# Smaller first loads over three queues, and another order of rounding and transposing in the first stretch of a two-layer decoder kernel

## The chip, the core and the metric

The kernel runs on one NeuronCore of one Trainium2 chip. Its engines work from queues of their own, each strictly in order: TensorE (PE: matmuls and transposes, with PEld its weight loads), VectorE (DVE), ScalarE (ACT), GpSimd (POOL) and SyncE (SP, which here only issues DMAs). ScalarE and GpSimd can issue DMAs too. The metric is device time in microseconds.

## The reference

Two layers of a decoder trunk over 512 tokens of width 1024: layer 0 mixes by sliding-window attention and a short gated convolution, layer 1 by chunked gated linear attention; each is followed by a gated MLP and a gated per-layer embedding. All of it is float32. What the change touches is the beginning of layer 0 alone:

```python
def _rms_norm(x, gain):
    xf = x.astype(jnp.float32)
    y = xf * lax.rsqrt(jnp.mean(xf * xf, axis=-1, keepdims=True) + RMS_EPS)
    return (y * gain.astype(jnp.float32)).astype(x.dtype)
...
    for i in range(DEPTH):
        j = i // 2
        h = _rms_norm(x, mix_norm[i])
        if i % 2 == 0:
            x = x + _attn_conv_mixer(h, cos, sin, hy_w_in[j], ...)
...
def _attn_conv_mixer(h, cos, sin, w_in, q_norm, k_norm, sinks, conv_w, w_out):
    b, s, _ = h.shape
    q, k, v, cb, cc, cx = _split(h @ w_in, HY_SPLITS)
```

The first thing computed is the part of `h @ w_in` that gives keys and values: 512 tokens by 256 columns, over 1024 inputs. The token's own factor of the norm is applied later; the gain is applied to x as it is prepared.

## The kernel before

**Products in three.** A float32 product is made of three matmuls on rounded operands (`mm3`, L166 to L168): each operand is cut into a high part (rounded, type fp32r) and the rest, a low part; the product is high x high, high x low, low x high. For weights, `cut` makes the parts: ScalarE copies with rounding (`wh`, L146), VectorE subtracts (`wl`, L147). For x, `split` does the same with the gain (ScalarE L112, VectorE L113; tiles `a`).

**The first stretch** (`mixer0`, L430 on). x arrives with tokens on partitions (`xin`, two tiles of 256 tokens) and is turned by TensorE into eight tiles of 128 inputs by 512 tokens: four 128x128 transposes for each, into a PSUM tile `ps` (`turned_in`, L477). From `ps` three things are made: the high part, the low part, and a plain copy `xT` that the layer needs later (`keep`, L492). The eight tiles are the eight blocks k of the sum of the key-value product: `keys_values(k)` is twelve matmuls of 128x256, three for each 128 tokens, into two PSUM tiles `pa` (L166 to L168; block 0, in another order of the same twelve, L465 to L468). Behind block 7 the query projection begins: 128x512 matmuls into `ps`, L166 to L168, and among its first a small transpose for the positions, L383.

**Order.** In this stretch the program fixes the order by hand (`manual_schedule`), for TensorE, VectorE and ScalarE. The tiles are turned in pairs (0, 1), (2, 3), (4, 5), (6, 7), each pair's eight transposes in one piece. Round c (1 to 3) turns pair c, keeps the pair before, prepares x tile 2c, the weights of pair c, and x tile 2c + 1, and multiplies block c. So the pair (2, 3) is prepared while block 1 is multiplied, (4, 5) at block 2, (6, 7) at block 3, and blocks 4 to 7 follow with all operands there.

**The start.** The loads of x and of the key-value weights go over SP (L441, L442), 256 KB each, four rounds of two pieces of x (256 inputs wide) and one of weights. ScalarE's queue loads the identity for the transposes (`cf`, L191) and the norm's gains (`vrow`, L217), which TensorE turns (L226) and VectorE copies (`vec`, L227) before any x can be split. Matmuls on a tile of ones (`idle`, L202) run on TensorE ahead of the first transposes (7) and ahead of the first products (3); their result goes nowhere.

Of the kernel before, what the change touches and what calls it, by code (L numbers as in the profile page):

```python
# [18 lines left out]
P = 128  # L19
# [37 lines left out]
class Kernel:  # L57
# [121 lines left out]
    def setup(self):  # L179
        nc, a = self.nc, self.a  # L180
        self.mhalf = self.cp.tile([P, 32], F32, name="mhalf")[:, :16]
        self.cf = self.cp.tile([P, P + 64 + 256], F32, name="cf")
        self.ident = self.cf[:, :P]
        ones = self.sq()[:, :P]
        self.ones_r = self.cp.tile([P, P], F32R, name="ones_r")
        self.nowhere = self.pa()
        with self.tc.manual_schedule(engines={ET.PE, ET.DVE, ET.Activation}):
            nc.vector.memset(ones, 1.0)
            nc.vector.tensor_copy(self.ones_r, ones)
            nc.vector.memset(self.mhalf, -0.5)  # L190
            nc.scalar.dma_start(self.ident, a["cst_f"][:, :P])  # L191
# [238 lines left out]
    def mixer0(self):  # L430
        nc, a, tc = self.nc, self.a, self.tc
        with tc.tile_pool(name="m0", bufs=1) as mp:
# [3 lines left out]
            kvr = self.raw(ND, 256)  # L436
# [16 lines left out]
            def keys_values(k):  # L453
                for t in range(NT):
                    self.mm3(
                        pkv[t], tok(k, t), wkv[k // 2](k % 2, 0, 256),
                        start=k == 0 and t % 2 == 0, stop=k == ND - 1 and t % 2 == 1,
                    )

            def first_keys_values():  # L460
                mm = nc.tensor.matmul
                wh, wl = wkv[0](0, 0, 256)
                for t in range(NT):
                    xh, _ = tok(0, t)
                    mm(pkv[t], xh, wh, start=t % 2 == 0, stop=False)  # L465
                    mm(pkv[t], xh, wl, start=False, stop=False)
                for t in range(NT):
                    mm(pkv[t], tok(0, t)[1], wh, start=False, stop=False)  # L468

            def turned_in(c):  # L470
                pss = [self.ps() for _ in range(2)]
                for u in range(2):
                    if c == 0 and u == 1:
                        self.vec0()
                    for m, ps in zip((2 * c, 2 * c + 1), pss):
# [6 lines left out]
            def weight(c):  # L482
                wkv.append(self.cut(kvr[:, 2 * c : 2 * c + 2, :], "a", (48, 16)))
# [6 lines left out]
            def keep(c, pss):  # L490
                return [
                    copy(self.xT[2 * c + u], pss[u]) for u, copy in enumerate((nc.scalar.copy, nc.vector.tensor_copy))  # L492
                ]
# [1668 lines left out]
```

## Time and profile before

| | us |
|---|---|
| three timed runs | 1194.11, 1194.17, 1194.54; median 1194.17 |
| the profiled execution | 1194.58 |
| its span on the core | 1192.8 |
| TensorE busy | 1187.1 (100%) |
| VectorE, ScalarE, GpSimd busy | 994.6 (83%), 685.4 (57%), 43.1 (4%) |
| first product of block 0, last product of block 7 (start) | 7.69, 21.50 |

The span is the time from the first to the last instruction; some 1.8 us of the execution lie around it. In the profile, matmuls are pipelined, so a matmul's duration is longer than the distance to the next one's start; rates are read from starts. The timeline's columns are start, duration, engine, line, operation, output<-inputs, count, and in brackets the idle time before it and what ended it. A row with a count above 1 starts with its first instruction and lasts to the end of its last. `a`, `ps`, `pa`, `wh`, `wl`, `raw` stand for all buffers of that name.

### The profile page before, as it was taken

How to read it: one execution, taken by the hardware profiler on the slowest of the kernel's cores; microseconds unless marked ns; L12 is line 12 of the kernel's file. 1: busy time of each engine (PE TensorE's matmuls, PEld its weight loads, DVE VectorE, ACT ScalarE, POOL GpSimd, SP SyncE). 2: the span in 40 equal slices, each digit the busy share in tenths (PEclk: the TensorE clock that was granted, in tenths of full speed). 3: DMA queues.
4: the chain of work that ended last, by engine and by line, in shares of the span. 5: the costliest groups of instructions: out<-in, count | busy, mean ns of one | idle time of the engine just before them, and what ended most of it. 6: DMA issues, size and time to landing. Idle time of an engine off the chain costs nothing.

```text
span 1192.8 us, 17964 instructions
## 1 busy us (share of the span) xinstructions
PE 1187.1 (100%) x7121; PEld 1038.9 (87%) x7121; DVE 994.6 (83%) x1571; ACT 685.4 (57%) x1116; POOL 43.1 (4%) x64
## 2 busy tenths in 40 slices
PE   9999999999999999999999999999999999999998
PEld 8887789999998889989988988889999999899887
DVE  6787687899999987789779866687999999986895
ACT  7566465655565744566563654555555656644764
POOL 2600000000000000000100000000000000000000
PEclk9999999999999999999999999999999999999999
DMA  7213322424232333232412222323242423423601
GB/s 224 82 62 91 90 71 71 142 71 142 71 118 95 119 129 98 97 106 70 142 60 71 74 69 71 107 65 112 72 141 71 142 72 122 135 89 98 212 1 71
DMA packets 110856, 117.62 MB, mean 99 GB/s; under 512 B 2824, under 2 KB 105794, under 8 KB 110772
## 3 DMA queue, kind: packets, MB, share of 16 engines
q1 hardware_dynamic: 109936, 115.88, 29.8%
q8 instruction: 56, 0.92, 0.3%
q0 software_dynamic: 560, 0.42, 0.3%
q14 instruction: 28, 0.23, 0.1%
q10 hardware_dynamic: 276, 0.18, 0.1%
HBM read 114.37 MB, written 2.10 MB: 98 GB/s over the span
## 4 chain that ended last, share of the span: by engine, by line
PE 100%; DVE 0%; ACT 0%; issue 0%
PE ps L166 14%; PE ps L167 14%; PE ps L168 14%; PE pa L167 7%; PE pa L166 7%; PE pa L168 7%; PE ps L912 6%; PE ps L914 6%; PE ps L913 6%; PE pa L912 2%; PE pa L914 2%; PE pa L913 2%; PE ps L1527 1%; PE ps L1526 1%; PE ps L1525 1%; PE pa L1866 1%
## 5 line engine op out<-in xcount | busy, mean ns | idle before, releaser
L146 ACT ACTIVATE wh<-raw 128x1024 fp32r<-128x1024 f32 (+4 forms) x144 | 143.6, 999 | 94.9 <-PE ps L167 61.7
L147 DVE TENSOR_TENSOR wl<-raw,wh 128x1024 fp32r<-128x1024 f32 (+4 forms) x144 | 166.0, 1153 | 28.9 <-ACT wh L146 28.1
L857 ACT ACTIVATE wh<-raw 128x1024 fp32r<-128x1024 f32 x84 | 89.3, 1063 | 119.6 <-DVE raw L881 63.8
L972 DVE SCALAR_TENSOR_TENSOR zt<-z,vfa,zt 128x510 f32<-128x510 f32 (+1 forms) x176 | 131.1, 747 | 5.3 <-ACT zt L970 4.7
L858 DVE TENSOR_TENSOR wl<-raw,wh 128x1024 fp32r<-128x1024 f32 x84 | 102.8, 1224 | 19.7 <-ACT wh L857 19.6
L970 ACT ACTIVATE zt<-z,vfb 128x512 f32<-128x512 f32 x88 | 71.0, 809 | 21.8 <-DVE four L1023 8.3
L166 PE MATMUL ps<-b,wh 128*128 128x512 f32 x192 | 76.2, 397 | 0.0
L167 PE MATMUL ps<-b,wh 128*128 128x512 f32 x192 | 75.0, 390 | 0.0
L168 PE MATMUL ps<-b,wl 128*128 128x512 f32 x192 | 74.9, 390 | 0.0
L912 PE MATMUL ps<-four,wh 128*128 128x256 f32 x256 | 71.5, 279 | 0.0
L914 PE MATMUL ps<-four,wl 128*128 128x256 f32 x256 | 71.0, 277 | 0.0
L913 PE MATMUL ps<-four,wh 128*128 128x256 f32 x256 | 70.8, 277 | 0.0
L167 PE MATMUL pa<-b,wh 128*128 128x512 f32 x176 | 69.0, 392 | 0.0
L167 PE MATMUL pa<-a,wh 128*128 128x512 f32 x176 | 69.0, 392 | 0.0
L166 PE MATMUL pa<-a,wh 128*128 128x512 f32 x176 | 69.0, 392 | 0.0
L166 PE MATMUL pa<-b,wh 128*128 128x512 f32 x176 | 69.0, 392 | 0.0
L168 PE MATMUL pa<-b,wl 128*128 128x512 f32 x176 | 68.4, 389 | 0.0
L168 PE MATMUL pa<-a,wl 128*128 128x512 f32 x176 | 68.4, 389 | 0.0
L166 PE MATMUL ps<-a,wh 128*128 128x512 f32 x128 | 50.6, 396 | 0.0
L167 PE MATMUL ps<-ul,wh 128*128 128x512 f32 x128 | 50.1, 391 | 0.0
L166 PE MATMUL ps<-uh,wh 128*128 128x512 f32 x128 | 50.1, 391 | 0.0
L912 PEld LDWEIGHTS ps<-four,wh 128*128 128x128 f32 x256 | 48.0, 188 | 2.3 <-ACT ps L937 0.5
(496 smaller groups left out, 3595.5 us busy)
## 6 DMA issues: line engine op xcount, KB each, us to landing
raw<-in_ffn_w_up_dram SPq DMA_DIRECT2D x44, 1024.0 KB, 5.1
raw<-in_ffn_w_down_dram SPq DMA_DIRECT2D x12, 1024.0 KB, 5.2
raw<-in_hy_w_in_dram SPq DMA_DIRECT2D x8, 1024.0 KB, 5.1
raw<-in_gla_w_in_dram SPq DMA_DIRECT2D x8, 1024.0 KB, 5.2
raw<-in_ffn_w_down_dram SPq DMA_DIRECT2D x8, 768.0 KB, 4.4
raw<-in_ple_w_gate_dram SPq DMA_DIRECT2D x6, 1024.0 KB, 5.2
raw<-in_hy_w_out_dram SPq DMA_DIRECT2D x16, 256.0 KB, 4.0
zt<-in_ffn_w_down_dram SPq DMA_DIRECT2D x8, 512.0 KB, 3.5
```

Of the source, the lines that this page charges most:

```text
L146: nc.scalar.activation(hv, v, AF.Copy)
L147: self.rest = nc.vector.tensor_tensor(lv, v, hv.bitcast(F32), ALU.subtract)
L166: mm(out, lh, rh, start=start, stop=False, **kw)
L167: mm(out, lh, rl, start=False, stop=False, **kw)
L168: return mm(out, ll, rh, start=False, stop=stop, **kw)
L857: nc.scalar.activation(h, src, AF.Copy)
L858: nc.vector.tensor_tensor(l, src, h.bitcast(F32), ALU.subtract)
L912: mm(out, wh, xh, start=first and j == 0, stop=False, **kw)
L913: mm(out, wh, xl, start=False, stop=False, **kw)
L914: mm(out, wl, xh, start=False, stop=j == ND // 2 - 1, **kw)
L970: nc.scalar.activation(y, z, AF.Identity, scale=w2[:, f : f + 1], bias=bb[:, f : f + 1])
L972: nc.vector.scalar_tensor_tensor(out=y[:, tap:], in0=z[:, : S - tap], scalar=w[:, f : f + 1], in1=y[:, tap:], op0=ALU.mult, op1=ALU.add,)
```

## The change

- **Loads.** The weights' first two blocks go over ScalarE's queue, one block each (128 KB), ahead of everything but the identity. The gains go over GpSimd's queue. x goes over SP in five rounds instead of four: the first two are 128 inputs wide (128 KB a piece), the others 256 as before.
- **Warm-up.** Four idle matmuls instead of seven ahead of the first transposes, one instead of three ahead of the first product.
- **Block 0.** Only tile 0 is turned ahead of it. Its weights (block 0 alone) are rounded ahead of x, and x's tile 0 is split in two halves of 256 tokens. Its twelve products are put in another order, with tile 1's four transposes after the first six.
- **Blocks 1 to 7.** A pair's eight transposes stand after the first six products of a block: (2, 3) in block 1, (4, 5) in block 2, (6, 7) in block 4. Block 1 is prepared after block 0's products, weights behind x. Round c then prepares pair c and multiplies blocks 2c and 2c + 1.

```diff
             nc.scalar.dma_start(self.ident, a["cst_f"][:, :P])
+            self.kvr = self.raw(ND, 256)
+            w_in = a["hy_w_in"][0].rearrange("(k p) n -> p k n", p=P)
+            for k in range(2):
+                nc.scalar.dma_start(self.kvr[:, k : k + 1, :], w_in[:, k : k + 1, 512:768])
             self.vec0 = self.load_vectors0()
-            self.idle(7)
+            self.idle(4)
...
-        finish = self.columns("vec0", [f(a["mix_norm"])], self.nc.scalar)
+        finish = self.columns("vec0", [f(a["mix_norm"])], self.nc.gpsimd)
...
-            for c in range(4):
-                cols = slice(c * 256, (c + 1) * 256)
+            for k0, k1 in ((0, 1), (1, 2), (2, 4), (4, 6), (6, 8)):
+                cols = slice(k0 * P, k1 * P)
...
-                nc.sync.dma_start(kvr[:, 2 * c : 2 * c + 2, :], w_in[:, 2 * c : 2 * c + 2, 512:768])
+                if k0 > 1:
+                    nc.sync.dma_start(kvr[:, k0:k1, :], w_in[:, k0:k1, 512:768])
...
+                products((0, 1), 0, wh)
+                products((0, 1), 0, wl)
+                products((2, 3), 0, wh)
+                (ps1,) = turned_in((1,))
+                products((0, 1), 1, wh)
+                products((2, 3), 0, wl)
+                products((2, 3), 1, wh)
...
-                pss = turned_in(0)
-                self.idle(3)
-                weight(0)
-                for u in range(2):
-                    operand(u, pss[u])
-                first_keys_values()
-                for c in range(1, 4):
-                    ahead = turned_in(c)
-                    keep(c - 1, pss)
-                    pss = ahead
-                    operand(2 * c, pss[0])
-                    weight(c)
-                    operand(2 * c + 1, pss[1])
-                    keys_values(c)
-                last = keep(3, pss)
-                for k in range(4, ND):
-                    keys_values(k)
+                (ps0,) = turned_in((0,))
+                self.idle(1)
+                hl = self.pair(self.fp, "a0", "a1")
+                xg.append(hl)
+                half = [slice(0, S // 2), slice(S // 2, S)]
+                part = lambda c: self.split([x[:, c] for x in hl], ps0[:, c], self.g_mix[0][:, :1])
+                weight(0, 1)
+                part(half[0])
+                part(half[1])
+                ps1 = first_keys_values()
+                operand(1, ps1)
+                weight(1, 2)
+                keep(0, ps0)
+                ahead = []
+                keys_values(1, lambda: ahead.extend(turned_in((2, 3))))
+                keep(1, ps1)
+                for c in range(1, 4):
+                    pss, ahead = ahead, []
+                    operand(2 * c, pss[0])
+                    weight(2 * c, 2 * c + 2)
+                    operand(2 * c + 1, pss[1])
+                    if c < 3:
+                        keys_values(2 * c, lambda: ahead.extend(turned_in((2 * c + 2, 2 * c + 3))))
+                    else:
+                        keys_values(2 * c)
+                    last = [keep(2 * c + u, pss[u]) for u in range(2)]
+                    keys_values(2 * c + 1)
```

TensorE's rows of before, from the end of block 0 to block 1's first products (`ps_172`, `ps_173`: tiles 2 and 3 of x; `wh_148`: the weights of blocks 0 and 1; `a_16_156`, `a_17_157`: high and low part of x's tile 1):

```order
L468 MATMUL pa_128<-wh_148,a_15_153 128x256 x2
L468 MATMUL pa_129<-wh_148,a_15_153 128x256 x2
L477 MATMUL ps_172<-cf,xin_111 128x128 x2
L477 MATMUL ps_173<-cf,xin_111 128x128 x2
L477 MATMUL ps_172<-cf,xin_112 128x128 x2
L477 MATMUL ps_173<-cf,xin_112 128x128 x2
L166 MATMUL pa_128<-wh_148,a_16_156 128x256
L167 MATMUL pa_128<-wl_149,a_16_156 128x256
L168 MATMUL pa_128<-wh_148,a_17_157 128x256
```

And of the change, from the middle of block 0 (`ps_157`: tile 1; `wh_172`, `wl_173`: the weights of block 1; `a_16_168`, `a_17_169`: x's tile 1):

```order
L473 MATMUL pa_129<-wh_143,a_11_141 128x256 x2
L492 MATMUL ps_157<-cf,xin_111 128x128 x2
L492 MATMUL ps_157<-cf,xin_112 128x128 x2
L473 MATMUL pa_128<-wh_143,a_12_142 128x256 x2
L473 MATMUL pa_129<-wl_144,a_11_141 128x256 x2
L473 MATMUL pa_129<-wh_143,a_12_142 128x256 x2
L166 MATMUL pa_128<-wh_172,a_16_168 128x256
L167 MATMUL pa_128<-wl_173,a_16_168 128x256
L168 MATMUL pa_128<-wh_172,a_17_169 128x256
```

Tile 1's transposes moved into block 0 and tiles 2 and 3's away from its end; between tile 1's transposes and the products that use it stand six products, where before eight transposes and block 0's twelve products stood.

ScalarE's rows of before behind the first weights (`a_14_152`, `a_16_156`, `a_20_184`, `a_24_192`: high parts of tiles 0 to 3):

```order
L146 ACTIVATE wh_148<-raw_113 128x512
L112 ACTIVATE a_14_152<-ps_132,vec_5_91 128x512
L112 ACTIVATE a_16_156<-ps_133,vec_5_91 128x512
L492 COPY xT_103<-ps_132 128x512
L112 ACTIVATE a_20_184<-ps_172,vec_5_91 128x512
L146 ACTIVATE wh_188<-raw_113 128x512
L112 ACTIVATE a_24_192<-ps_173,vec_5_91 128x512
```

And of the change (`a_11_141`: tile 0 in halves, `a_16_168`: tile 1, `a_22_200`, `a_26_208`: tiles 2 and 3):

```order
L146 ACTIVATE wh_143<-raw_87 128x256
L112 ACTIVATE a_11_141<-ps_132,vec_6_94 128x256 x2
L112 ACTIVATE a_16_168<-ps_157,vec_6_94 128x512
L146 ACTIVATE wh_172<-raw_87 128x256
L507 COPY xT_103<-ps_132 128x512
L112 ACTIVATE a_22_200<-ps_183,vec_6_94 128x512
L146 ACTIVATE wh_204<-raw_87 128x512
L112 ACTIVATE a_26_208<-ps_184,vec_6_94 128x512
```

Block 1's weights, which came with block 0's before, are now a row of their own, behind tile 1's high part; the pair (2, 3) keeps its order of high part, weights, high part.

More of the change, by code (lines that the diff above doesn't have):

```diff
@@ L451, in mixer0, with keys_values, products, turned_in @@
             wkv = []
-            def keys_values(k):
+            def keys_values(k, then=None):
                 for t in range(NT):
                     self.mm3(
-                        pkv[t], tok(k, t), wkv[k // 2](k % 2, 0, 256),
+                        pkv[t], tok(k, t), wkv[k](0, 0, 256),
                         start=k == 0 and t % 2 == 0, stop=k == ND - 1 and t % 2 == 1,
                     )
+                    if then and t == 1:
+                        then()
             def first_keys_values():
-                mm = nc.tensor.matmul
                 wh, wl = wkv[0](0, 0, 256)
[L463 to L471, printed above, removed]
+                started = set()
+                def products(ts, part, w):
+                    for t in ts:
+                        nc.tensor.matmul(pkv[t], tok(0, t)[part], w, start=t % 2 == 0 and t not in started, stop=False)
+                        started.add(t)
+                products((0, 1), 0, wh)
[5 more added lines that the diff above has]
+                products((2, 3), 1, wh)
+                return ps1
+            def turned_in(ms):
+                pss = [self.ps() for _ in ms]
                 for u in range(2):
-                    if c == 0 and u == 1:
+                    if ms[0] == 0 and u == 1:
                         self.vec0()
-                    for m, ps in zip((2 * c, 2 * c + 1), pss):
+                    for m, ps in zip(ms, pss):
                         for t in (2 * u, 2 * u + 1):
```

13 lines of the change are left out of this document (6 added, 7 removed).

## The prediction

> **What bounds the kernel now.** I read the page's engine totals first, then its chain of work that ended last.
>
> ```profile
> PE 1187.1 (100%) x7121; PEld 1038.9 (87%) x7121; DVE 994.6 (83%) x1571; ACT 685.4 (57%) x1116; POOL 43.1 (4%) x64
> ...
> PE 100%; DVE 0%; ACT 0%; issue 0%
> ```
>
> TensorE works through the whole span, and the chain lies on it. The two orders of instructions differ, on every engine, from the start to a few matmuls into the query projection; from there on they are the same row for row. So what counts is one moment: when TensorE has issued the last of the 96 key-value products and goes on to the query projection. Everything behind it shifts by as much. The table by stretches shows the stage (columns: stretch, its length, busy time and count on PE, PEld, DVE, ACT and POOL, granted clock, DMA share, GB/s).
>
> ```profile
> 5.00:7.70 2.70, 2.70 (x12) 2.09 (x11) 1.44 (x3) 1.89 (x3) 0.00 (x0) 1.00 1.00 321
> 7.70:21.90 14.20, 14.20 (x123) 14.05 (x121) 11.54 (x18) 12.23 (x20) 6.82 (x17) 1.00 0.90 272
> ```
>
> The DMA engines are full until TensorE is under way, and from 7.7 us TensorE has no gap. The timeline of TensorE (start, duration, engine, line, operation, count) gives the rates.
>
> ```profile
> 1.31 3.35 PE L202 MATMUL pa<-ones_r 128*128 128x512 f32 x7 [1.31 <-DVE mhalf L190]
> 4.47 1.05 PE L477 MATMUL ps<-cf,xin 128*128 128x128 f32 x4
> 5.45 0.28 PE L226 MATMUL pa<-cf,vrow 16*128 16x16 f32 x1
> 5.67 1.11 PE L477 MATMUL ps<-cf,xin 128*128 128x128 f32 x4
> 6.43 1.42 PE L202 MATMUL pa<-ones_r 128*128 128x512 f32 x3
> 7.69 0.28 PE L465 MATMUL pa<-wh,a 128*128 128x256 f32 x1
> 7.81 0.28 PE L466 MATMUL pa<-wl,a 128*128 128x256 f32 x1
> ...
> 8.63 0.62 PE L468 MATMUL pa<-wh,a 128*128 128x256 f32 x4
> 9.09 1.03 PE L477 MATMUL ps<-cf,xin 128*128 128x128 f32 x8
> ...
> 11.38 1.04 PE L477 MATMUL ps<-cf,xin 128*128 128x128 f32 x8
> ...
> 21.50 0.28 PE L168 MATMUL pa<-wh,a 128*128 128x256 f32 x1
> 21.71 0.22 PE L383 MATMUL pa<-cf,pos_f 4*128 4x4 f32 x1
> ```
>
> A product takes 0.118 us of TensorE, a transpose 0.11 (8 transposes and 12 products: 11.38 - 9.09 = 2.29). The 128x512 warm-up matmuls start 0.43 to 0.45 apart and the first transposes 0.21 to 0.25, about half speed, up to the last of the three at about 7.4; the product at 7.69 is at full speed. (The column of the granted clock says 1.00 throughout; here the spacing tells more.) Block 0 ends at 9.09, and 24 transposes and 84 products follow without a gap: 12.53 us, to 21.50 + 0.12 = 21.62.
>
> **Why there is no gap before.** ScalarE and VectorE prepare a tile pair in this order (the two engines' timelines):
>
> ```profile
> 5.77 0.63 ACT L146 ACTIVATE wh<-raw 128x512 fp32r<-128x512 f32 x1 [2.54 <-DMA raw<-in_hy_w_in_dram]
> ...
> 9.94 0.69 ACT L112 ACTIVATE a<-ps,vec 128x512 fp32r<-128x512 f32 x1 [1.45 <-PE ps L477]
> 10.53 0.62 ACT L146 ACTIVATE wh<-raw 128x512 fp32r<-128x512 f32 x1
> ...
> 16.21 1.06 ACT L146 ACTIVATE wh<-raw 128x1024 fp32r<-128x1024 f32 x1
> ```
>
> ```profile
> 5.77 0.17 DVE L227 COPY vec<-pa 128x16 f32<-128x16 f32 x1 [4.49 <-PE pa L226]
> ...
> 10.66 0.75 DVE L113 SCALAR_TENSOR_TENSOR a<-ps,vec,a 128x512 fp32r<-128x512 f32 x1 [1.54 <-ACT a L112]
> 11.33 0.68 DVE L147 TENSOR_TENSOR wl<-raw,wh 128x512 fp32r<-128x512 f32 x1
> ...
> 18.21 1.22 DVE L147 TENSOR_TENSOR wl<-raw,wh 128x1024 fp32r<-128x1024 f32 x1
> ```
>
> From a pair's transposes to its rounded-off weights `wl` (11.33 + 0.68 = 12.01) some 2 us pass. Before, the products of block 1 stand there, ready long ago; the pair (2, 3) is multiplied only from the next round on. The chain costs nothing.
>
> **The change part by part.** First the start. The loads:
>
> ```profile
> 0.73 0.45 ACTq L191 DMA_DIRECT2D cf<-in_cst_f_dram  x1
> 1.21 0.49 ACTq L217 DMA_DIRECT2D vrow<-in_mix_norm_dram  x1
> ```
>
> ```profile
> xin<-in_x_dram SPq DMA_DIRECT2D x2, 256.0 KB, 3.4
> raw<-in_hy_w_in_dram SPq DMA_DIRECT2D x1, 256.0 KB, 4.0
> cf<-in_cst_f_dram ACTq DMA_DIRECT2D x1, 64.0 KB, 3.0
> ```
>
> A queue issues one load in 0.48 us. The identity and the first x piece (issued at 0.73) land 3.0 to 3.4 later: transposes from about 3.85. The second x piece and the first weights (issued at 1.21, 128 KB) land 3.0 to 4.0 later, 4.2 to 5.2; I take 4.5, since fewer bytes lie ahead of them. The gains go over POOL, which no load did this early before; the later ones there (the DMA list of the whole run) land between these two:
>
> ```profile
> vrow<-in_ffn_conv_w_dram POOLq DMA_DIRECT2D x6, 22.0 KB, 2.3
> vrow<-in_gla_o_norm_dram POOLq DMA_DIRECT2D x1, 1.0 KB, 4.8
> ```
>
> So 3.0 to 5.5; most such rows are near the lower end, and I take "there by 4.3". TensorE at half speed: two transposes 3.85 to 4.28, the gains' transpose to 4.5, two more to 4.93, one warm-up to 5.4. VectorE's copy is done at 4.28 + 0.28 + 0.17, about 4.8. A 256-wide operation lies below the 512-wide by half the step to 1024: `wh` 0.62 - 0.22 = 0.40, x's high part 0.47, `wl` 0.42. `wh` runs 4.5 to 4.9, x's first half 4.8 to 5.3: first product at 5.4, 2.3 us sooner. What of this stays? At 0.21 us each, 6 products and tile 1's 4 transposes reach 7.5; there I keep the full speed where it came before, so 6 more products take 0.71: block 0 ends at 8.2. Against 9.09, with the same 24 transposes and 84 products to come, that is **0.89 us gained**.
>
> The clock is where a rule of the Trainium skill speaks against the change. The page "TensorE: Matmul & The Clock Gate", section "Part 1: The HAM clock gate (the "warmup" mystery)", has the array at half speed until a free-running window of about 3.4 us was busy. The rows agree in kind: matmuls from 1.31, full speed after 7.4. Five warm-up matmuls instead of ten, with a pause from 3.1 to 3.85, could by that page bring full speed up to a window later. By the rows' 7.5 the sum below is 1196.0; with a window lost it is the 1196.5 of the second rival.
>
> Then **gap 1**. Tile 1's last transpose starts at 7.3 and ends 0.42 later: 7.7. ScalarE's next row is x's high part (0.69, to 8.4), and only behind it the weights of block 1, landed long before. VectorE makes x's low part (next start after 0.67: 9.1) and `wl` (0.42): 9.52. From there to the matmul:
>
> ```profile
> 613.56 0.40 DVE L1825 TENSOR_TENSOR F<-kT,qT 128x256 f32<-128x256 f32 x1
> ...
> 614.01 0.30 PEld L1831 LDWEIGHTS pa<-F,ones_r 128*128 128x128 f32 x2 [0.45 <-DVE F L1825]
> ```
>
> 0.05 us to the weight load and up to the load's length behind it; I take 0.15 in all. TensorE takes its rows in order, the second of block 1 needs `wl`: 9.67. It stands idle from 8.2 to 9.55: **1.35 us**.
>
> **Gap 2.** Block 1's first six products end at 10.26; the eight transposes of the pair (2, 3) stand there. Tile 2 is whole with the sixth: 10.26 + 0.55 + 0.27 = 11.08. ScalarE: high part, then weights, 11.1 + 0.59 + 0.62 = 12.31. VectorE: low part from 11.82, `wl` 12.49 to 13.18, plus 0.15. TensorE has used up two transposes and six products by 11.85 and waits until 13.21: **1.36 us**. Block 2 follows its own pair at once now; that lag is what the old order had.
>
> No third gap: tiles 4 and 6 have two transposes, six products and the whole of block 3 or 5 behind them (0.22 + 19 x 0.118 = 2.46 with the first product itself), against the same chain of 2.52. That 0.06 I leave out. The x and weight pieces of the later blocks have the same bytes ahead of them as before, over DMA engines that were full already, and block 2 starts later than it did; a piece that still came late would add its lateness. ScalarE's two more issues end at 2.2, and its table load is done before the first weights land.
>
> Sum: 13.21 + 72 products (8.50) + 16 transposes (1.76) = 23.47 against 21.62: **+1.85 us** (2.71 of gaps less 0.89, and rounding). The query weights behind it: ScalarE's high part of tile 7, a copy as long and the 1024-wide weights (0.59 + 0.59 + 1.06), then VectorE's 1.22, make 3.46 from some 0.75 before block 6 begins, so 2.7 after it; 24 products cover 2.8. If they didn't, the difference would be added. The profiled run was 1194.58 in all, so 1196.4; by the median of 1194.17, **1196.0 us**. A measurement of this kernel tells about 0.2%, 2.4 us, from no change, so this falls just inside.
>
> **The rivals.** *The gaps do not open.* If TensorE found block 1 and 2 ready (transposes now stand amid products, and before shows 14.2 us without a gap), only 0.89 gained would be left: 1193.3; with one gap of the two, 1194.6. Against it: the rows stand in order, and the chain's four durations are measured. Decides: `wl` of block 1 ready before 8.2. 0.12.
>
> *Full speed comes a window later.* Priced from rows: the last 6 products of block 0 at 0.21 take 0.55 more, but gap 1 hides it (ready time 9.67 depends on the transposes); block 1's six then cost 0.55 more: 1196.5. Decides: half speed still at 9.6. It is the result that the page above allows. 0.15. Should full speed come sooner, at 5.8, eight of the first ten instructions take 0.9 instead of 1.7: 1195.2, inside my case.
>
> *The gains arrive last.* At 5.5 from POOL (row 4.8) the high part starts at 6.1 instead of 4.8, less the warm-up's and transposes' share done meanwhile, about 0.7 net at block 1: 1196.7, slower by over 0.2%. For it: the only load whose kind of queue is new. Against: rows of 2.3. Decides: landing after 4.3. 0.10.
>
> **How the numbers follow.** My case 0.60, the three 0.12, 0.15, 0.10, others 0.03. Range: earlier speed and a shorter wait (0.05 instead of 0.15, twice) take 1.0 off: 1194.9. Weights at 5.2 (0.4) with late speed (0.5) and a wait of 0.25 (0.2) add 1.1: 1197.2. Slower than 1196.6: a quarter of my case, half of the late clock, most of the late gains, 0.30. Faster than 1191.8: block 0 at full speed from 5.4 (1.86) with no gap would end at 19.79, 1192.3, so 0.02.
>
> **What would show it.** Right: first product near 5.4, last one near 23.4; TensorE idle over 1 us before L167's first product of block 1 and of block 2, both ended by `wl` from VectorE; none before block 4 and 6; everything behind shifted alike. Wrong: no PE idle in 8 to 14 us; the gains' transpose waiting for POOL's load; products 0.21 apart after 9; or a shift that is not the last product's.

## The result, and the profile after

The changed kernel takes 1198.37 us in the median of nine runs (1197.55 to 1198.72), the kernel before 1194.81 beside it (nine runs, 1194.11 to 1196.98). The ratio is 1.0025, with a 95% interval from 1.0016 to 1.0033: slower by some 3.0 us by the ratio of the runs' times and by 3.56 by the medians, where 1.85 was forecast. The forecast time of 1196.0 and its range, 1194.9 to 1197.2, miss it. The profiled execution took 1198.71, with a span of 1196.8.

The page of the changed kernel, engine totals and the chain's shares by engine:

```profile
PE 1188.1 (99%) x7116; PEld 1038.3 (87%) x7116; DVE 993.8 (83%) x1573; ACT 684.3 (57%) x1118; POOL 43.6 (4%) x65
...
PE 95%; DVE 3%; DMA 1%; ACT 0%; issue 0%; ACTq 0%; POOLq 0%
```

The chain has left TensorE: some of it runs over VectorE now, and over a DMA. The table by stretches of the changed kernel (columns as for before) shows where TensorE rests:

```profile
6.50:9.85 3.35, 3.32 (x16) 3.18 (x16) 0.97 (x2) 1.08 (x3) 0.00 (x0) 1.00 1.04 350
9.85:11.10 1.25, 0.54 (x3) 0.19 (x1) 1.14 (x3) 0.86 (x3) 0.00 (x0) 1.00 1.05 361
11.10:13.39 2.29, 2.29 (x19) 2.25 (x19) 0.56 (x2) 0.74 (x2) 0.65 (x6) 1.00 1.07 398
13.39:14.78 1.39, 0.54 (x3) 0.19 (x2) 1.39 (x3) 1.39 (x3) 1.39 (x5) 1.00 0.93 354
14.78:25.00 10.22, 10.22 (x87) 10.22 (x88) 8.05 (x12) 7.35 (x12) 4.45 (x9) 1.00 0.41 77
```

Block 0 fills the first row. The second is gap 1, TensorE's rest at the start of block 1, and the fourth is gap 2, at the start of block 2; in the last TensorE has no rest. The timeline of TensorE (start, duration, line, operation, count, idle time before and its releaser):

```profile
5.07 0.28 PE L230 MATMUL pa<-cf,vrow 16*128 16x16 f32 x1 [0.86 <-DMA vrow<-in_mix_norm_dram]
5.28 0.69 PE L492 MATMUL ps<-cf,xin 128*128 128x128 f32 x2
...
6.53 0.80 PE L473 MATMUL pa<-wh,a 128*128 128x256 f32 x2
...
8.15 1.06 PE L492 MATMUL ps<-cf,xin 128*128 128x128 f32 x4
...
9.61 0.40 PE L473 MATMUL pa<-wh,a 128*128 128x256 f32 x2
...
11.10 0.39 PE L167 MATMUL pa<-wl,a 128*128 128x256 f32 x1 [0.43 <-DVE wl L147]
11.33 0.28 PE L168 MATMUL pa<-wh,a 128*128 128x256 f32 x1
...
14.78 0.39 PE L167 MATMUL pa<-wl,a 128*128 128x256 f32 x1 [0.48 <-DVE wl L147]
...
24.89 0.28 PE L168 MATMUL pa<-wh,a 128*128 128x256 f32 x1
```

Block 0 ends at 9.61 + 2 x 0.118 = 9.85, 0.76 later than before's 9.09. Gap 1 costs 1.24 (from 9.85 to the third product of block 1 at 11.33, less the two products between), gap 2 by the same reading 1.38. That is 3.38, and the last product starts 3.39 later (24.89 against 21.50).

The gains were loaded over GpSimd's queue (its timeline, then the list of DMA loads with the size and the time from issue to landing):

```profile
1.26 0.70 POOL L221 DMA_DIRECT2D vrow<-in_mix_norm_dram  x1 [0.81 <-POOLq L2172]
```

```profile
vrow<-in_mix_norm_dram POOLq DMA_DIRECT2D x1, 8.0 KB, 3.8
```

The issue began at 1.26, not at 0.73 as the first ones of ScalarE and SyncE, and the gains landed 3.8 us later, at 5.0.

ScalarE and VectorE around tile 0 and tile 1 in the changed kernel (their two timelines):

```profile
4.87 0.42 ACT L146 ACTIVATE wh<-raw 128x256 fp32r<-128x256 f32 x1 [1.13 <-DMA raw<-in_hy_w_in_dram]
6.00 0.47 ACT L112 ACTIVATE a<-ps,vec 128x256 fp32r<-128x256 f32 x1 [0.72 <-PE ps L492]
7.03 0.47 ACT L112 ACTIVATE a<-ps,vec 128x256 fp32r<-128x256 f32 x1 [0.55 <-DVE a L113]
9.24 0.69 ACT L112 ACTIVATE a<-ps,vec 128x512 fp32r<-128x512 f32 x1 [1.74 <-PE ps L492]
9.83 0.41 ACT L146 ACTIVATE wh<-raw 128x256 fp32r<-128x256 f32 x1
```

```profile
5.39 0.17 DVE L231 COPY vec<-pa 128x16 f32<-128x16 f32 x1 [4.10 <-PE pa L230]
...
6.51 0.48 DVE L113 SCALAR_TENSOR_TENSOR a<-ps,vec,a 128x256 fp32r<-128x256 f32 x1 [0.61 <-ACT a L112]
...
9.96 0.75 DVE L113 SCALAR_TENSOR_TENSOR a<-ps,vec,a 128x512 fp32r<-128x512 f32 x1 [1.95 <-ACT a L112]
10.63 0.42 DVE L147 TENSOR_TENSOR wl<-raw,wh 128x256 fp32r<-128x256 f32 x1
```

The two halves of tile 0 stand one behind the other: ScalarE's first half waits for TensorE although the gains have been copied for 0.4 us, and its second half waits 0.55 for VectorE's first. Gap 1 is the chain of the forecast: transposes, high part 9.24, low part 9.96, `wl` 10.63, product 11.10.

Behind the first stretch everything is later by the same 3.4 us up to 851 us of before's time. There this execution loses 0.8 more. TensorE's and ScalarE's rows of the changed kernel, and ScalarE's row at the same place before:

```profile
855.83 0.39 PE L936 MATMUL ps<-four,wh 128*128 128x256 f32 x1 [0.54 <-ACT ps L961]
```

```profile
836.17 1.06 ACT L881 ACTIVATE wh<-raw 128x1024 fp32r<-128x1024 f32 x1 [1.37 <-DMA raw<-in_ffn_w_up_dram]
```

```profile
831.78 1.04 ACT L857 ACTIVATE wh<-raw 128x1024 fp32r<-128x1024 f32 x1
```

A piece of the second MLP's weights landed 1.4 us too late for ScalarE. Of the fifteen profiles other than before's, eight keep the shift of their first stretch to the end, and seven lose 0.4 to 1.4 us more behind it, most of it at 237 us, at 852 us or at both.

### The profile page after: what moved, and what is told of

It reads as the page before. It is cut to its first block, busy times and chain, and to the rows that moved or that the text cites. A ratio compares the mean times of both kernels' runs of the same rounds, so it can differ in the third digit from the quotient of the medians.

```text
span 1196.8 us, 17961 instructions
## 1 busy us (share of the span) xinstructions
PE 1188.1 (99%) x7116; PEld 1038.3 (87%) x7116; DVE 993.8 (83%) x1573; ACT 684.3 (57%) x1118; POOL 43.6 (4%) x65
## 4 chain that ended last, share of the span: by engine, by line
PE 95%; DVE 3%; DMA 1%; ACT 0%; issue 0%; ACTq 0%; POOLq 0%
PE ps L166 14%; PE ps L167 14%; PE ps L168 14%; PE pa L167 7%; PE pa L166 7%; PE pa L168 7%; PE ps L936 6%; PE ps L938 6%; PE ps L937 6%; PE pa L936 2%; PE pa L938 2%; PE pa L937 2%; PE ps L1551 1%; PE ps L1549 1%; PE ps L1550 1%; DVE zt L996 1%
## 5 line engine op out<-in xcount | busy, mean ns | idle before, releaser
L146 ACT ACTIVATE wh<-raw 128x1024 fp32r<-128x1024 f32 (+5 forms) x145 | 143.7, 993 | 89.4 <-PE ps L167 59.8
L147 DVE TENSOR_TENSOR wl<-raw,wh 128x1024 fp32r<-128x1024 f32 (+5 forms) x145 | 165.5, 1142 | 26.2 <-ACT wh L146 25.6
```

The costliest lines, as they stand in the source:

```text
L146: nc.scalar.activation(hv, v, AF.Copy)
L147: self.rest = nc.vector.tensor_tensor(lv, v, hv.bitcast(F32), ALU.subtract)
```

## The experiments

Times of a run are compared with the kernel before on the same chip (medians 1194.34 to 1194.97). An interval is about 1 us wide to either side, so a shift of the last product by less can't be told from the times; there the traces decide. The table gives starts from TensorE's timelines, each from one profiled execution; "third of block 1" is the product behind gap 1, where there is one. The forecast's row is worked out from the prediction: 5.4 + 6 x 0.21 = 6.66, 9.67 + 0.12, and 23.47 - 0.12.

| kernel | gains' transpose | first product | tile 1's transposes | third of block 1 | last product |
|---|---|---|---|---|---|
| before | 5.45 | 7.69 | | | 21.50 |
| forecast | 4.28 | 5.40 | 6.66 | 9.79 | 23.35 |
| changed, first profile | 5.07 | 6.53 | 8.15 | 11.33 | 24.89 |
| changed, second profile | 4.46 | 5.92 | 7.54 | 10.72 | 24.29 |
| gains on ScalarE's queue | 4.22 | 6.63 | 8.24 | 11.42 | 24.97 |
| seven warm-ups ahead | 5.03 | 6.49 | 8.12 | 11.29 | 24.85 |
| no halves | 5.15 | 6.83 | 8.28 | 11.62 | 25.38 |
| seven and three warm-ups | 5.03 | 6.97 | 7.87 | 10.59 | 24.16 |
| better start | 5.03 | 6.71 | 7.87 | 10.58 | 24.15 |
| two PSUM tiles | 4.86 | 5.99 | 7.37 | 10.54 | 24.10 |
| two PSUM tiles, gains on ScalarE | 5.22 | 6.35 | 7.73 | 10.90 | 24.46 |

**The old order of blocks 1 to 7.** The changed loads, start and block 0 stay; round c turns pair c, prepares it and multiplies block c, as before.

```diff
+                pss = [ps0, ps1]
                 for c in range(1, 4):
-                    pss, ahead = ahead, []
+                    ahead = turned_in((2 * c, 2 * c + 1))
...
                     operand(2 * c, pss[0])
                     weight(2 * c, 2 * c + 2)
                     operand(2 * c + 1, pss[1])
-                    if c < 3:
-                        keys_values(2 * c, lambda: ahead.extend(turned_in((2 * c + 2, 2 * c + 3))))
...
+                    keys_values(c)
...
+                for k in range(4, ND):
+                    keys_values(k)
```

> The changed kernel's loads, warm-up and block 0, but with the old lag: the pair (2, 3) is turned ahead of block 1, (4, 5) ahead of block 2, (6, 7) ahead of block 3, and blocks 4 to 7 follow with all operands ready. If the missing round between a pair's transposes and its products makes the gaps ahead of blocks 1 and 2 (1.25 and 1.38 us in the profile after), the second gap goes wholly and the first shrinks to about 0.4 us (eight transposes now stand in it): last key-value product near 22.6 instead of 24.89, time about 2.2 us below the changed kernel, still some 1 us above the kernel before. If the late start (gains, clock) is what makes the products wait, the gaps stay and the last product stays near 24.9.

Measured: 1195.78 us, ratio 1.0013 (1.0004 to 1.0022). Both gaps are gone; TensorE's timeline goes from block 0 into the next pair's transposes and on without a wait:

```profile
9.86 1.04 PE L492 MATMUL ps<-cf,xin 128*128 128x128 f32 x8
10.65 0.36 PE L166 MATMUL pa<-wh,a 128*128 128x256 f32 x1
10.86 0.28 PE L167 MATMUL pa<-wl,a 128*128 128x256 f32 x1
```

The last product starts at 22.27, 2.62 sooner than in the changed kernel. What is left, 0.77 over before, belongs to the start, and block 0 still ends at 9.86.

**The gains on ScalarE's queue, ahead of the weights.**

```diff
+            self.vec0 = self.load_vectors0()
             self.kvr = self.raw(ND, 256)
...
-            self.vec0 = self.load_vectors0()
...
-        finish = self.columns("vec0", [f(a["mix_norm"])], self.nc.gpsimd)
+        finish = self.columns("vec0", [f(a["mix_norm"])], self.nc.scalar)
```

> The changed kernel with the gains' load back on ScalarE's queue, ahead of the two weight pieces. If the gains over POOL start the products late (they landed at about 5.0, TensorE waited 0.86 us for them), the gains' transpose comes at 4.3 to 4.6, the first product 0.4 to 0.7 sooner, and the last product at 24.2 to 24.5. The weight pieces are issued 0.5 later but landed at 4.87 with a second to spare. If the loads' bytes and not the queue set their landing, the gains come at 5.0 again and nothing moves.

Measured: 1198.17 us, ratio 1.0034 (1.0021 to 1.0046). The gains landed 2.4 us after their issue (the list of DMA loads), but the weights behind them on the queue were late (ScalarE's timeline):

```profile
vrow<-in_mix_norm_dram ACTq DMA_DIRECT2D x1, 8.0 KB, 2.4
```

```profile
1.22 0.49 ACTq L221 DMA_DIRECT2D vrow<-in_mix_norm_dram  x1
...
1.80 0.41 ACTq L196 DMA_DIRECT2D raw<-in_hy_w_in_dram  x1
...
5.79 0.42 ACT L146 ACTIVATE wh<-raw 128x256 fp32r<-128x256 f32 x1 [2.57 <-DMA raw<-in_hy_w_in_dram]
```

One place later on the queue, issued 0.6 later, the weights were taken up at 5.79, where the two profiles of the changed kernel have 4.87 and 4.27. So they were the last to come, and the first product came no sooner (6.63).

**Seven warm-up matmuls ahead of the transposes instead of four.**

```diff
-            self.idle(4)
+            self.idle(7)
```

> The changed kernel with seven warm-up matmuls instead of four ahead of the first transposes (one ahead of the first product, as changed). If the fewer matmuls delayed full speed (spacing halves at 9.3 us after, at 7.4 before), full speed comes at 7.4 to 7.7 again and the last product 0.7 to 0.9 sooner, near 24.1; the extra matmuls end at 4.3 and the gains come at 5.0, so they delay nothing. If the moment is chance, it comes anywhere between 6 and 10 and the mean of the runs doesn't move.

Measured: 1197.17 us, ratio 1.0023 (1.0012 to 1.0033). The last product starts at 24.85, and full speed came no sooner: the last products of block 0 are still 0.21 apart (two from 9.82 to 10.25).

```profile
9.82 0.63 PE L473 MATMUL pa<-wh,a 128*128 128x256 f32 x2
10.25 0.53 PE L166 MATMUL pa<-wh,a 128*128 128x256 f32 x1
```

**Weights ahead of x in block 1 and in every pair.**

```diff
+                weight(1, 2)
                 operand(1, ps1)
-                weight(1, 2)
...
+                    weight(2 * c, 2 * c + 2)
                     operand(2 * c, pss[0])
-                    weight(2 * c, 2 * c + 2)
```

> The changed kernel with the weights rounded ahead of x in blocks 1 and in every pair, not in block 0 alone. If the gaps are the chain high part, weights' high part, weights' low part, taking the weights out of it leaves high part and low part of x: gap 1 falls by about 0.5 us, gap 2 by about 0.75, last product near 23.7. If the gaps are ended by something else (x landing, tiles), they stay.

Measured: 1196.89 us, ratio 1.0018 (1.0009 to 1.0028). The last product starts at 23.10. TensorE no longer rests ahead of block 1, whose first products still ran at half speed here, and gap 2 shrinks to one short wait, now for x's low part:

```profile
13.11 0.39 PE L168 MATMUL pa<-wh,a 128*128 128x256 f32 x1 [0.28 <-DVE a L113]
```

The gains came at 4.44 here; the changed kernel's second profile, with gains at 4.46, has its last product at 24.29. Like against like, having the weights ready ahead is worth 1.19, less than half of that profile's two gaps of 1.33 and 1.38. The rest is the wait for x itself: its low part of tile 1 is done by 10.1, and the third product of block 1 starts at 10.15.

**Before, with the changed kernel's warm-ups.** Loads and order of before; profiled once with timed runs, and a second time.

```diff
-            self.idle(7)
+            self.idle(4)
...
-                self.idle(3)
+                self.idle(1)
```

> The kernel before, with only the changed kernel's number of warm-up matmuls (four and one instead of seven and three); loads, order and preparation stay. If full speed comes with a fixed stretch of time in which TensorE was kept busy, the pauses now left ahead of the first product put it back from 7.5 us to 9.5 to 10.9: the first product stays within 0.5 us of before's 7.69 (its operands set it), all of block 0 runs at half rate, the last product starts at 22.3 to 23.0 instead of 21.50, and the time is 0.8 to 1.5 us over before. Rival: full speed comes by time alone; then the last product starts at 21.0 to 21.6 and the time is before's or up to 0.5 us less.

> A second look at before with four and one warm-up matmuls. If the moment of full speed hangs on a stretch that runs free of the kernel, it can differ from the first look's 9.0 us by up to 3.4 us with the same first product (6.7): full speed at 9.0 to 12.4, and the last product at 21.7 to 22.9. Rival: the kernel alone sets it; then both come again within 0.2 us.

Measured: 1196.59 us in the median, ratio 1.0013 (1.0004 to 1.0023), spread over 2.8 us (1195.01 to 1197.77); the second profile 1194.90 (one run). In the first profile block 0 ran at half speed and the products came 0.21 apart, as expected:

```profile
6.73 0.58 PE L465 MATMUL pa<-wh,a 128*128 128x256 f32 x1
7.11 0.42 PE L466 MATMUL pa<-wl,a 128*128 128x256 f32 x1
7.33 0.42 PE L465 MATMUL pa<-wh,a 128*128 128x256 f32 x1
```

But the last product starts at 21.70 and 21.87, not at 22.3 or later: before's three warm-ups had themselves held the first product up, to 7.69, and with fewer of them, and weights that landed 0.3 sooner than before's, it came at 6.73 and 6.87. So the two effects nearly cancel in these profiles. The timed runs lie 1.6 us over before by the ratio, which the shift of 0.2 and the 0.6 lost later in the first profile don't explain. Full speed came at 9.0 and 9.2; the two agree too well to show that the moment wanders.

**The old order and before's warm-ups.** The first experiment with seven and three.

```diff
-            self.idle(4)
+            self.idle(7)
...
-                self.idle(1)
+                self.idle(3)
```

> The kernel of the first experiment (the changed kernel's loads and block 0, with the old order from block 1 on), with before's number of warm-up matmuls, seven and three, so that TensorE is busy up to the first product. If the pauses put the clock back, full speed now comes before 8.2 us, the first product starts at 6.2 to 6.8, the last one at 21.1 to 21.7 (22.27 in the first experiment), and the time is within 0.6 us of before. Rival: full speed comes late for another reason; then the last product starts at 22.2 or later.

Measured: 1194.77 us, ratio 1.0001 (0.9991 to 1.0010). TensorE's timeline:

```profile
5.25 0.50 PE L492 MATMUL ps<-cf,xin 128*128 128x128 f32 x2
5.50 0.94 PE L206 MATMUL pa<-ones_r 128*128 128x512 f32 x3
...
21.70 0.28 PE L168 MATMUL pa<-wh,a 128*128 128x256 f32 x1
```

Transposes 0.125 apart from 5.25: full speed is there. The last product starts 0.57 sooner than in the first experiment, and the time is before's again. With the order and the warm-ups of before, no loss is left that the times could show; the last product is 0.20 behind before's.

**No halves.** Tile 0 split whole.

```diff
-                part(half[0])
-                part(half[1])
+                operand(0, ps0)
```

> The changed kernel with x's tile 0 split whole instead of in two halves; all else stays. If the halves run one behind the other (ScalarE, VectorE, ScalarE, VectorE), they bring little: the first product comes 0 to 0.3 us later, the last product starts within 0.3 us of the changed kernel's 24.89, and the time is the same. Rival: the halves do bring block 0 forward; then the last product comes 0.4 us or more later.

Measured: 1198.24 us, ratio 1.0029 (1.0018 to 1.0041), the changed kernel's time. The first product comes 0.30 later; the last one 0.49, more than expected, in an execution in which full speed came only at 12.0. In the timed runs the halves brought nothing that could be measured.

**A combined try:** old order; the first two weight blocks on SP, one behind each of the first two x rounds; gains on ScalarE's queue; seven and two warm-ups; tile 0 whole; tile 1's transposes after the first four products; block 1's weights rounded ahead of x's tile 1.

```diff
-            for k in range(2):
-                nc.scalar.dma_start(self.kvr[:, k : k + 1, :], w_in[:, k : k + 1, 512:768])
...
-                if k0 > 1:
+                if True:
                     nc.sync.dma_start(kvr[:, k0:k1, :], w_in[:, k0:k1, 512:768])
...
-                self.idle(1)
...
+                self.idle(2)
...
+                weight(1, 2)
                 operand(1, ps1)
-                weight(1, 2)
```

> A try at a kernel better than both: the old order from block 1 on; weights in single blocks for the first two, on SP's queue behind the first x pieces; the gains on ScalarE's queue; seven and two warm-up matmuls; tile 0 split whole; tile 1's transposes after the first four products. If start, clock and order are understood, first product 6.0 to 6.8, full speed before 8.2, no gap in the blocks, last product at 20.9 to 21.5 against before's 21.50, and a time 0 to 0.6 us below before. Rival: the single weight block lands as late as the double one did, or the clock is put back by a pause; then the last product starts at 22.0 or later and the time is 0.5 us or more over before.

Measured: 1195.16 us, ratio 1.0003 (0.9994 to 1.0012). The first stretch did nearly what it should: first product at 6.04, last product at 21.17, 0.33 ahead of before. One wait is left: the transposes ahead of block 2 start 0.36 after the products before them, held by a late piece of x. Part of the gain is chance: full speed came at 4.2 here, and only at 7.4 in the run below that has the same start, whose first product stands at 6.71. The profiled execution then gave 1.35 away, most of it at the weights piece already met (ScalarE's timeline):

```profile
832.99 1.06 ACT L868 ACTIVATE wh<-raw 128x1024 fp32r<-128x1024 f32 x1 [1.66 <-DMA raw<-in_ffn_w_up_dram]
```

No kernel here beats the one before by what can be measured.

**The changed kernel with before's warm-ups.**

```diff
-            self.idle(4)
+            self.idle(7)
...
-                self.idle(1)
+                self.idle(3)
```

> The changed kernel with before's number of warm-up matmuls, seven and three; all else stays. If the late full speed of the changed kernel comes from the pauses ahead of its first product, full speed is there before 8.2 us, block 0 ends at 8.6 to 9.1 instead of 9.85, both gaps of about 1.3 us stay, the last product starts at 23.7 to 24.3 (24.89 in the changed kernel) and the time is 0.6 to 1.2 us below the changed kernel's. Rival: gap 1 swallows what block 0 gains; then the last product starts at 24.6 or later.

Measured: 1197.28 us, ratio 1.0020 (1.0011 to 1.0030). TensorE's timeline:

```profile
6.97 0.40 PE L473 MATMUL pa<-wh,a 128*128 128x256 f32 x2
7.21 0.40 PE L473 MATMUL pa<-wl,a 128*128 128x256 f32 x2
...
10.36 0.39 PE L167 MATMUL pa<-wl,a 128*128 128x256 f32 x1 [0.43 <-DVE wl L147]
```

Full speed at 6.9, block 0's end at 9.02, gaps of 1.33 and 1.38, last product at 24.16: each as expected. The time, expected 0.6 to 1.2 us under the changed kernel's, can't be told from it by the ratios. The first product is 0.44 later than in the changed kernel's first profile, yet block 1 comes 0.74 sooner: tile 1's transposes and products at full speed more than pay for it.

**The changed order with the combined try's start** (its loads, seven and two warm-ups, tile 0 whole).

```diff
-            for k in range(2):
-                nc.scalar.dma_start(self.kvr[:, k : k + 1, :], w_in[:, k : k + 1, 512:768])
...
-            self.idle(4)
+            self.idle(7)
...
-        finish = self.columns("vec0", [f(a["mix_norm"])], self.nc.gpsimd)
+        finish = self.columns("vec0", [f(a["mix_norm"])], self.nc.scalar)
...
-                if k0 > 1:
+                if True:
...
-                self.idle(1)
...
+                self.idle(2)
...
-                part(half[0])
-                part(half[1])
+                operand(0, ps0)
```

> The changed kernel's order of blocks, with the start of the combined try: the first weights on SP's queue behind the first x pieces, the gains on ScalarE's queue, seven and two warm-up matmuls, tile 0 whole. If the forecast failed by its start alone, this start gives what the forecast put in: first product at 5.9 to 6.6, block 0's end at 7.8 to 8.6, gaps of 1.2 to 1.6 us ahead of blocks 1 and 2, the last product at 23.0 to 23.8 (forecast 23.35), and a time 1.5 to 2.4 us over before. Rival: the gaps grow by what the start gains; then the last product starts at 24.3 or later.

Measured: 1197.65 us, ratio 1.0024 (1.0014 to 1.0033). The start was not the better one: first product at 6.71, block 0's end at 9.02, last product at 24.15. The test of the forecast's start failed for want of the start; the gaps, 1.32 and 1.37, stayed as they were.

**The changed kernel, profiled a second time.**

> A second look at the changed kernel, for what of its start comes again. By a free-running stretch full speed may come anywhere from 8.5 to 12.0 us (9.3 in the first look); the gains' transpose at 4.4 to 5.2; gap 1 hides most of both, so the last product starts within 0.6 us of 24.89. Rival: the start repeats within 0.2 us in each of these.

Measured: 1197.29 us (one run). TensorE's timeline:

```profile
4.46 0.28 PE L230 MATMUL pa<-cf,vrow 16*128 16x16 f32 x1 [0.15 <-DMA vrow<-in_mix_norm_dram]
...
5.92 0.80 PE L473 MATMUL pa<-wh,a 128*128 128x256 f32 x2
...
7.54 1.05 PE L492 MATMUL ps<-cf,xin 128*128 128x128 f32 x4
```

The gains came 0.61 sooner, and the first product, tile 1's transposes, block 1 and the last product all came 0.60 to 0.61 sooner. Gap 1 hides nothing of late gains, against what was expected. Full speed came at 8.5. The gains were again issued at 1.26, and landed 3.2 us later instead of 3.8.

**Tile 0 in two PSUM tiles, one for each half.** So far the split of the missing 1.54 us is read from waits alone; this run and the next one test it.

```diff
-                (ps0,) = turned_in((0,))
+                pa0, pb0 = self.ps(), self.ps()
+                ps0 = (pa0, pb0)
...
-                part = lambda c: self.split([x[:, c] for x in hl], ps0[:, c], self.g_mix[0][:, :1])
+                part = lambda u: self.split([x[:, half[u]] for x in hl], ps0[u][:, half[u]], self.g_mix[0][:, :1])
...
-                keep(0, ps0)
+                for u in range(2):
+                    nc.scalar.copy(self.xT[0][:, half[u]], ps0[u][:, half[u]])
```

The plain copy of tile 0 is made from two tiles now, both halves on ScalarE, behind block 0.

> The changed kernel with tile 0 of x turned into two PSUM tiles, one for each half; all else stays. If the first half's high part stood back for the transposes of the other half because both lie in one PSUM tile, it now starts as soon as the gains are copied: 0.1 us behind the end of VectorE's copy of the gains, where the changed kernel has 0.4 us, and the first product comes 0.8 to 1.2 us behind the gains' transpose (1.46 in both looks so far). The step from the first product to tile 1's transposes grows from 1.62 by as much, if ScalarE's second half still waits for VectorE's first half; then the last product keeps its 16.7 us behind tile 1's transposes and the time stays within 0.5 us of the changed kernel's. Rival: the halves are free of each other too; then the step is 1.3 us, and the time 0.5 to 0.8 us less.

Measured: 1197.35 us, ratio 1.0025 (1.0015 to 1.0034). ScalarE's timeline, then TensorE's:

```profile
5.39 0.88 ACT L112 ACTIVATE a<-ps,vec 128x256 fp32r<-128x256 f32 x2 [0.31 <-DVE vec L231]
```

```profile
4.86 0.28 PE L230 MATMUL pa<-cf,vrow 16*128 16x16 f32 x1 [0.63 <-DMA vrow<-in_mix_norm_dram]
...
5.99 0.73 PE L473 MATMUL pa<-wh,a 128*128 128x256 f32 x2
...
7.37 1.06 PE L492 MATMUL ps<-cf,xin 128*128 128x128 f32 x4
```

Both waits are gone: the first half waits for the gains alone, and the second follows it at once. So one PSUM tile for both halves had made both. From the gains' transpose to the last product are 19.24 us, against 19.82 and 19.83 in the two profiles of the changed kernel: 0.58 for the two waits. The rival was right on the halves; in the ratio of times the 0.58 can't be told.

**And the gains on ScalarE's queue, between the two weight pieces.**

```diff
-            for k in range(2):
-                nc.scalar.dma_start(self.kvr[:, k : k + 1, :], w_in[:, k : k + 1, 512:768])
+            nc.scalar.dma_start(self.kvr[:, 0:1, :], w_in[:, 0:1, 512:768])
             self.vec0 = self.load_vectors0()
+            nc.scalar.dma_start(self.kvr[:, 1:2, :], w_in[:, 1:2, 512:768])
...
-        finish = self.columns("vec0", [f(a["mix_norm"])], self.nc.gpsimd)
+        finish = self.columns("vec0", [f(a["mix_norm"])], self.nc.scalar)
```

> As the run with two PSUM tiles, and the gains go over ScalarE's queue between the two weight pieces, not over GpSimd's. If the late gains and the one PSUM tile are what the forecast's start missed, the gains' transpose stands at 4.2 to 4.6, the first product at 5.2 to 5.7 (forecast 5.4), tile 1's transposes at 6.8 to 7.4, and the last product 16.7 us behind these, at 23.5 to 24.1 (forecast 23.35); the time is 0.8 to 1.4 us less than the changed kernel's. Rival: the first weights land late and set the start; then the first product stands at 5.9 or later and the last one at 24.3 or later.

Measured: 1197.62 us, ratio 1.0026 (1.0016 to 1.0035). The rival's marks are met (first product at 6.35, last one at 24.46), but not by its cause: the weights came in time (`wh` at 4.51), and the gains were late again, issued at 1.74 (ScalarE's timeline) and waited for at 5.22 (TensorE's).

```profile
1.74 0.48 ACTq L221 DMA_DIRECT2D vrow<-in_mix_norm_dram  x1
```

```profile
5.22 0.28 PE L230 MATMUL pa<-cf,vrow 16*128 16x16 f32 x1 [0.99 <-DMA vrow<-in_mix_norm_dram]
```

So the lateness is not GpSimd's own. The gains, 8 KB, could be used 3.5 us after their issue here. By the lists of DMA loads they landed 3.1 to 3.8 after their issue at 1.26 on GpSimd's queue (nine profiles), and 2.4 to 2.5 after theirs at 1.22 as the second load of ScalarE's (three profiles). Why they come later behind the weights is open. From the gains' transpose on the run repeats the one with two tiles: 19.24 to the last product, though full speed came not before 9.9 here and at 8.6 there.

## Why the prediction was wrong

**Right: what bounds the kernel.** The last key-value product shifted by 3.39 us, and everything behind it by 3.4 up to 851 us.

**Right: both gaps, their cause and their size.** Forecast 1.35 and 1.36, both ended by `wl` from VectorE; measured 1.24 and 1.38, or 1.33 and 1.38 where block 0 ran faster, with VectorE's `wl` as the releaser each time. Restoring the old order takes both away. From block 1's third product to the last one the forecast has 23.35 - 9.79 = 13.56 us; measured 24.89 - 11.33 = 13.56. No third gap opened. From tile 1's transposes to that third product it has 3.13; measured 3.18. The first rival, that the gaps do not open, is refuted.

**Wrong: the start.** The forecast let tile 1's transposes begin at 6.66; they began at 8.15, and the last product came 1.54 late. Three terms make this up:
- The gains, "there by 4.3" over a queue whose early landing the trace did not show. Their transpose stood at 5.07 instead of 4.28: 0.79 of the 1.54; in the second profile 0.18. The forecast's 3.0 to 5.5 are the rows' 2.3 and 4.8 behind an issue at 0.7; GpSimd's issue began at 1.26, which is 0.5 of it. The third rival named late gains with a chance of 0.10 and priced a landing at 5.5 at 0.7, by letting part of the delay be hidden; the two profiles of the changed kernel show that it passes on whole.
- The first half of x, let start at 4.8, as soon as the gains were copied, with two of its tile's transposes yet to come; and the second half, taken to follow with no wait. Neither holds in one PSUM tile: 0.58 by the run with two tiles.
- The remaining 0.17 lies by the run with two tiles in the six products ahead of tile 1's transposes, 1.38 instead of 1.26, and in the chain from there to block 1, 3.17 instead of 3.13.

With block 0 ending at 9.85 instead of 8.2, the forecast gain of 0.89 became a loss of 0.76, and the two gaps came on top of it. So the failed step is the sum for the start: its landing of the gains, and its overlap of tile 0's halves with the other half's transposes and with each other. Even the changed kernel with seven and three warm-ups ends block 0 only at 9.02, against 9.09.

**The clock.** Full speed came at 9.3 in the first profile, not at 7.5: the second rival's case, though short of its mark of 9.6. It cost next to nothing against the forecast, since that had already put half speed on everything up to tile 1's last transpose; what followed at half speed lay under gap 1, as that rival said (two PSUM tiles, full speed at 8.6 or not before 9.9: 19.24 both times from the gains to the last product). Against before it did cost: with seven and three warm-ups, at full speed from 6.9, the way from tile 1's transposes to the third product of block 1 is 2.72 instead of 3.18.

**The range.** It took a step for late weights, late speed and longer waits, but left late gains to a rival and had no room for waits inside tile 0. (Its ends lie 0.1 outside its own sums of 1.0 and 1.1.) The time of 1198.37 is 2.37 over the forecast's 1196.0, and the start is only 1.54 of it: another 0.64 is the base, since the forecast added to a median of 1194.17 from three runs, and nine runs of the same kernel give 1194.81. Behind the first stretch, 0.8 us more went at the weights piece in the profiled execution, and nothing in the second profile, so the timed runs carry it in part; how often is open, as is why that piece comes late.

## What to carry to other kernels

A transpose moved in among products saves nothing unless what is made from it has as much work standing behind it as its chain takes; add that chain up over all engines, ahead of moving it: here 3.2 us from tile 1's first transpose to the third product of block 1 in the changed kernel. Splitting a tile to start sooner needs split buffers too: halves in one PSUM tile waited for each other's writer and reader. And of the first loads price the smallest as carefully as the largest, since the last to land sets the start. One place further back on ScalarE's queue cost about 0.5 us in the issue, but 0.9 to 1.5 us at the weights' landing and some 1.5 at the gains'.

## What the runs showed of the hardware that was not expected

The moment of full speed, read from spacings of matmuls, falls in two groups, a division made after the runs. In the five profiles with seven warm-ups and little rest up to the first product it came at 4.2, 5.3, 6.9, 7.4 and 7.5 us; in the eleven with a pause ahead of it, be it with seven warm-ups, between 8.5 and 12.0. The groups are 3.3 and 3.5 us wide. The Trainium skill's page "TensorE: Matmul & The Clock Gate", section "Part 1: The HAM clock gate (the "warmup" mystery)", has a free-running window of about 3.4 us that must have been busy. The width of the groups agrees with that; that a pause costs just one window is not shown, since the groups lie 4.3 to 4.5 us apart. The same page puts the scatter of the transition from run to run at half a microsecond either way. Two profiles of one kernel lay 0.8 and 0.2 apart here. But three kernels of the first group, with seven warm-ups and the same starts on TensorE up to 5.25 us within 0.02, reached full speed at 5.3, 6.9 and 7.4, which is more than that.

The granted clock stands at 1.00 in all rows of the table by stretches, the half-speed ones too.

A load of 8 KB issued within the first 2 us landed 3.1 to 3.8 us after its issue on GpSimd's queue (nine profiles), could be used after 3.5 on ScalarE's behind a weights piece (one), and landed after 2.4 to 2.5 there ahead of any weights (three). Its place on the queue counted for more than the kind of queue.
